# A two-layer hybrid block on one core: four more feed-forward chunks by seven block products, raw weights in half tiles, and a turn of the activations without steps

## The chip, the cores and the metric

The kernel runs on one core of one Trainium2 chip. The metric is the device time of one execution in microseconds (us), as the median of several runs; lower is better. The names of the engines are those of the profile: PE is TensorE (matmuls), PEld its weight loads, DVE is VectorE, ACT is ScalarE, POOL is GpSimd, SP is SyncE, which here issues nearly all DMA transfers in one order.

## What is computed

Two layers over 256 tokens of width 1024, all in float32. Each layer has two feed-forward nets, and between them a mixer and a cross attention that the change touches only through its smaller pieces. Every part is followed by a residual sum and a layer norm:

```python
def swiglu(x, w_gate, w_up, w_down):
    return (jax.nn.silu(x @ w_gate) * (x @ w_up)) @ w_down

for l in range(DEPTH):                      # DEPTH = 2
    h = layer_norm(ALPHA * h + 0.5 * swiglu(h, ffn1_gate[l], ffn1_up[l], ffn1_down[l]), ...)
    ...                                     # mixer, then cross attention
    h = layer_norm(ALPHA * h + 0.5 * swiglu(h, ffn2_gate[l], ffn2_up[l], ffn2_down[l]), ...)
```

The hidden width of a net is 2816, so a net has five chunks of 512 hidden columns (chunks 0 to 4) and a last one of 256 (chunk 5). There are four nets, called net 1 (ffn1 of the first layer) to net 4 (ffn2 of the second) below.

## The kernel before, in words

**Precision.** Every float32 factor is kept as two tiles of a faster matmul type, a high part and the rest. `split` (L60) makes them: ACT casts the source into the high part (L61), then DVE subtracts it from the source and writes the low part (L62). A product is three matmuls: high by high, high by low, low by high (`mm_rows`, L130; the matmul itself is L106). For weights the two parts are 128x1024 tiles named whi and wlo. One such pair is called a *piece* here. There are 8 buffers of whi and of wlo, so that a piece can only be cast when PE has done with the piece eight before it.

**Weights.** `load` (L64) brings 1 MB (128x2048) at a time into a tile named raw, of which there are three, by one DMA from SP, and splits it into two pieces. A raw tile is free again when both its pieces are split. The down weights of chunks 0 to 4 are read so that a partition takes neighbouring rows (`strewn`, L78).

**A net** (`ffn`, L376) goes through the chunks in order (L639). In a usual chunk (`hidden`, L484, and `first`, L424, for chunk 0) gate and up are each 8 blocks of 128 rows, in 4 pieces each; a piece serves 12 matmuls. With the two token tiles that is 96 matmuls of 512 columns. SiLU and the product of gate and up (`activate` L401, `gated` L404) leave an activation of tokens by columns, which `turn` (L411) brings into columns by tokens: four DMAs deal it among the partitions (L415), two DVE transposes of 32x32 blocks turn it (L418), and `split` makes its two parts (ah, al). After chunk c come the down products of chunk c-2, second half, and of chunk c-1, first half (`both`, L631: two pieces and 24 matmuls each). The last three slabs of down weights run token tile by token tile in `finish` (L292) with the layer norm.

**Seven products.** In nets 2 to 4 chunk 3 goes through `by_seven` (L515): token tiles, halves of the input rows, and gate and up form a 2x2 block product, which is done with 7 block products in place of 8, each of 12 matmuls: 84 in place of 96. Each of the 7 needs 2 pieces, which serve 6 matmuls each, so there are 14 pieces in place of 8. Four of the block products take sums of weight blocks. They are made in place, one after the other, by DVE (L544, 8 additions of 128x1024). Sums of x are made beforehand by `blocks_of_x` (L497) in a tile named quarters and put into kTh and kTl; in the code it stands behind chunk 1. The results are put together by DVE (L566). The raw blocks lie in: a tile "spare" that the quarters have used before (w00), the tiles of the layer norm's factors (w01), and two raw tiles (w11, w10).

**What sets the order.** Each engine runs its own instructions strictly in the order of the built program. That order is made by a scheduler at build time, from the code's order and its own estimate of costs; it is fixed when the kernel runs. SP's transfers too are one queue in that order.

Of the kernel before, what the change touches and what calls it, by code (L numbers as in the profile page):

```python
# [17 lines left out]
P = 128  # L18
# [28 lines left out]
def model(ctx: ExitStack, tc: tile.TileContext, t: dict, out: bass.AP):  # L47
# [16 lines left out]
    def load(src, k0, nk, c0, ncol, fine=False, strewn=False):  # L64

        hi, lo, todo = [], [], []
        step = 2048 // ncol
        for a in range(k0, k0 + nk, step):  # L70
            raw = wp.tile([P, 2048], F32, tag="raw", name="raw", bufs=3)
            raw = raw.rearrange("p (k c) -> p k c", c=ncol)
            half = step // 2
            part = 1 if fine else step
            for b in range(0, step, part):
                loads.append(nc.sync.dma_start(
                    raw[:, b : b + part, :],
                    src[:, c0 : c0 + ncol].rearrange("(p k) c -> p k c", p=P)[:, a + b : a + b + part, :]  # L78
                    if strewn
                    else src[(a + b) * P : (a + b + part) * P, c0 : c0 + ncol].rearrange("(k p) c -> p k c", p=P),  # L80
                ))
            for s in range(2):
                h = wp.tile([P, 1024], F32R, tag="whi", name="whi", bufs=8)
                w = wp.tile([P, 1024], F32R, tag="wlo", name="wlo", bufs=8)
                h = h.rearrange("p (k c) -> p k c", c=ncol)
                w = w.rearrange("p (k c) -> p k c", c=ncol)
                r = raw[:, s * half : (s + 1) * half, :]
# [65 lines left out]

    jdn = cst.tile([P, P], F32, name="jdn")
# [24 lines left out]
    def load_memory(mp, behind):  # L179
        m = [mp.tile([P, 4, 8, 32], F32, tag="m", name="m", bufs=2) for _ in range(2)]  # L180
# [23 lines left out]
    rows = cst.tile([P, P], F32, name="rows")  # L204
# [10 lines left out]
    def small_parameters(op):  # L215
        nc.gpsimd.memset(rows, 0.0)
# [13 lines left out]
        mf = op.tile([P, NT, len(narrow), 64], F32, name="mf", bufs=1)  # L230
# [61 lines left out]
    def finish(mm, y, scale, gb, last=False, flip=False):  # L292
# [6 lines left out]
        for i in range(NT):  # L299
# [8 lines left out]
            for c in pieces:  # L308
# [6 lines left out]
                else:  # L315
                    mm(
                        i, n, slice(0, 512), None,
                        None if last or not i or not n else lambda: transposed(h[0], 0, xTh, xTl),
# [21 lines left out]
        return lambda: transposed(h[1], 1, xTh, xTl, jdn if flip else idn)  # L340

    def project_back(slabs, late, gb, scale, between=lambda: None):
# [30 lines left out]
        return finish(tail, y, scale, gb)  # L373


    def ffn(l, name, n, pend=None, last=False, early=None):  # L376
        gate, up, down = (t[f"{name}_{x}"][l] for x in ("gate", "up", "down"))
        with tc.tile_pool(name="ffn", bufs=2, reuse_waits="tile") as fp:
# [21 lines left out]

            def activate(s, i, og):  # L401
                nc.scalar.activation(halves(s[:, i, :]), sums(og), AF.Silu)

            def gated(s, i, ou):  # L404
                v = halves(s[:, i, :])
                nc.vector.tensor_tensor(v, sums(ou), v, op=ALU.mult)
# [4 lines left out]
            def turn(s):  # L411
# [4 lines left out]
                for i in range(NT):  # L416
                    d = fp.tile([P, 4, P], F32, tag="up", name="square")
                    nc.vector.transpose(  # L418
                        d.rearrange("p k (i b) -> p b k i", b=4), x[:, :, i, :].rearrange("p b (j k) -> p b k j", k=4)
# [4 lines left out]
            def first():  # L424
# [5 lines left out]
                if pend is None:  # L430
# [8 lines left out]
                    with tc.manual_schedule(engines={E.Activation, E.DVE, E.PE}):  # L439
# [8 lines left out]
                        transposed_half(h[0], 0, 0, xTh, xTl)  # L448
                        busy(1)
                        split(*wg.todo[0])  # L450
                        transposed_half(h[0], 0, 1, xTh, xTl)
# [3 lines left out]
                        transposed_half(h[1], 1, 0, xTh, xTl)  # L455
                        group(1, 0)
                        split(*wg.todo[2])
                        transposed_half(h[1], 1, 1, xTh, xTl)
# [38 lines left out]
            def blocks_of_x():  # L497

                d = fp.tile([P, 4, 4 * P], F32, tag="spare", name="quarters", bufs=1)
                q = [d[:, n, :].rearrange("p (k t) -> p k t", t=P) for n in range(4)]  # L500
# [14 lines left out]
            def by_seven(c0, bx):  # L515
                def quarter(m, j, halves_of):
                    for b, r in enumerate(halves_of):
                        n = r.shape[1]
                        k = 4 * j + b * n
                        loads.append(nc.sync.dma_start(  # L520
                            r, m[k * P : (k + n) * P, c0 : c0 + CHUNK].rearrange("(k p) c -> p k c", p=P)
                        ))
                    return [r[:, 2 * h : 2 * h + 2, :] for h in range(2) for r in halves_of[:1]] if n == 4 else halves_of

# [3 lines left out]
                def raw():  # L528
                    return rows_by_columns(wp.tile([P, 2048], F32, tag="raw", name="raw", bufs=3))
# [4 lines left out]
                w01 = quarter(up, 0, [  # L534
                    rows_by_columns(wp.tile([P, DM], F32, tag=g, name="raw")) for g in ("lng", "lnb")
                ])
                w11 = quarter(up, 1, [raw()])
                w10 = quarter(gate, 1, [raw()])

                def parts_of(r, plus=None):  # L540
                    hi, lo = [], []
                    for i in range(2):
# [4 lines left out]
                        h, w = (x.rearrange("p (k c) -> p k c", c=CHUNK) for x in (h, w))  # L547
# [14 lines left out]
                def half_sum():  # L562
                    return halves(fp.tile([P, 4, P], F32, tag="up", name="half").rearrange("p k t -> p (k t)"))

                def put(o, a, op, b):
                    nc.vector.tensor_tensor(o, a, b, op=op)  # L566

                s = activations()
                g = [halves(s[:, i, :]) for i in range(NT)]
                o = [acc((P, CHUNK)) for _ in range(4)]  # L570
                run(o[0], part_of_x(0, 0), parts_of(w00))
                nc.scalar.copy(g[0], sums(o[0]))
# [3 lines left out]
                put(e, sums(o[1]), ALU.add, g[0])  # L576
                run(o[3], bx[2], parts_of(w01, w11))
                put(g[1], sums(o[3]), ALU.add, e)
                f = half_sum()
                put(f, sums(o[2]), ALU.subtract, g[1])  # L580
                put(e, sums(o[2]), ALU.subtract, e)
# [12 lines left out]
                put(g[0], g[0], ALU.mult, e)  # L594
                return turn(s)

            def last_hidden(c0):
# [11 lines left out]
                split(ah[:, 0:2, :], al[:, 0:2, :], s)  # L609
# [11 lines left out]
            sevens = (3,) if early is None else ()  # L621
# [17 lines left out]
            for c, (c0, ncol) in enumerate(chunks):  # L639
# [7 lines left out]
                if c == 1 and sevens:  # L647
                    bx = blocks_of_x()
                if c == (max(sevens) + 1 if sevens else 1):

                    with tc.issue_after(loads[-1].ins) if early is not None else nullcontext():
                        gb = ln_params(l, n)
                        rest = early(fp) if early is not None else ()
# [19 lines left out]
            return finish(tail, ys, 0.5, gb, last=last, flip=name == "ffn1")  # L673
# [27 lines left out]
    def mixer(l, fill):  # L701
        w_in = t["w_in"][l]
        with tc.tile_pool(name="mix", bufs=1, reuse_waits="tile") as mp:
# [284 lines left out]
            return project_back([slab(a) for a in (0, 6, 2, 4)], 3, gb, 1.0)  # L988


    def attention(l, pend):
        scale = (DM // HEADS) ** -0.5
        with tc.tile_pool(name="att", bufs=1, reuse_waits="tile") as ap:
# [108 lines left out]
            return project_back([slab(a) for a in (0, 2, 4, 6)], 3, gb, 1.0, others)  # L1102
# [40 lines left out]
```

## Time and profile before

| what | us |
|---|---|
| median of 3 runs (lowest, highest) | 1081.91 (1081.46, 1082.29) |
| the profiled execution's own time | 1082.44 |
| its span in the profile | 1080.7 |
| PE busy | 1071.4 (99%) |
| DVE busy | 908.4 (84%) |
| ACT busy | 592.8 (55%) |
| mean traffic of the DMA engines | 215 GB/s |

Times inside the profile count from the start of the span. A group of instructions is given with its line, engine, operation, "out<-in" by the program's tile names, a shape and a count; then its busy time in all, the mean duration of one in ns, and the idle time of the engine just before it with what ended that. A row of a timeline has start, length, engine, line, operation and count, and in brackets the idle time before it. Two DVE instructions in a row overlap a little, so that the distance from start to start is shorter than the duration of one.

### The profile page before, as it was taken

The numbers are of one execution on the slowest core, as the hardware profiler recorded it, in microseconds if no ns is written. First come the engines' busy times: TensorE is split into PE (matmuls) and PEld (weight loads), VectorE is DVE, ScalarE is ACT, GpSimd is POOL, SyncE is SP. The second block draws the span as 40 slices with busy tenths as digits, with TensorE's granted clock in tenths as the row PEclk, the third lists the DMA queues.
The fourth block names the chain that finished last, engine by engine and source line by source line (L and its number), as shares of the span: only waits on it lengthen the run. The fifth ranks groups of instructions, "written<-read, shape, count | busy, mean of one in ns | idle before, by whom it ended". The sixth has DMA issues, their size and how long they took to land.

```text
span 1080.7 us, 15689 instructions
## 1 busy us (share of the span) xinstructions
PE 1071.4 (99%) x6015; PEld 947.5 (88%) x6015; DVE 908.4 (84%) x1198; ACT 592.8 (55%) x828; POOL 61.0 (6%) x113
## 2 busy tenths in 40 slices
PE   9999999999999999999999999999999999999997
PEld 7888888989899888888888888898898998888886
DVE  6678677998988898998697998798989889889885
ACT  6456553766457455556365465456764664645650
POOL 9500001000000000000000000010000000000000
PEclk9999999999999999999999999999999999999999
DMA  9986764754476387288468459656536664773761
GB/s 325 289 293 203 249 223 153 237 196 165 167 263 204 123 295 269 96 275 286 156 234 282 166 166 329 229 165 241 174 122 231 240 228 154 255 253 109 260 236 39
DMA packets 122715, 231.86 MB, mean 215 GB/s; under 512 B 6352, under 2 KB 45552, under 8 KB 117520
## 3 DMA queue, kind: packets, MB, share of 16 engines
q1 hardware_dynamic: 120848, 228.48, 63.1%
q0 software_dynamic: 1216, 1.20, 0.4%
q10 hardware_dynamic: 576, 1.18, 0.3%
q8 instruction: 47, 0.77, 0.3%
q14 instruction: 28, 0.23, 0.1%
HBM read 216.15 MB, written 1.05 MB: 201 GB/s over the span
## 4 chain that ended last, share of the span: by engine, by line
PE 99%; DMA 0%; DVE 0%; issue 0%; DVEq 0%
PE acc L106 65%; PE dn L106 30%; PE acc L170 1%; PE dn L845 1%; DMA h<-in_x_dram 0%; PE dn L904 0%; PE dn L903 0%; PE dn L893 0%; PE acc L969 0%; PE dn L810 0%; PE dn L437 0%; DVE h L334 0%; DVE h L330 0%; DVE st L322 0%; DVE h L314 0%
## 5 line engine op out<-in xcount | busy, mean ns | idle before, releaser
L62 DVE TENSOR_TENSOR wlo<-raw,whi 128x1024 fp32r<-128x1024 f32 (+1 forms) x390 | 460.8, 1207 | 91.0 <-ACT whi L61 81.1
L61 ACT CAST whi<-raw 128x1024 fp32r<-128x1024 f32 (+1 forms) x390 | 391.2, 1040 | 258.3 <-PE dn L106 128.4
L106 PE MATMUL acc<-whi,xT 128*128 128x512 f32 x1192 | 359.7, 380 | 0.0
L106 PEld LDWEIGHTS acc<-whi,xT 128*128 128x128 f32 x1192 | 225.2, 189 | 32.1
L106 PE MATMUL acc<-wlo,xT 128*128 128x512 f32 x596 | 225.9, 379 | 0.0
L106 PE MATMUL acc<-xT,whi 128*128 128x512 f32 x576 | 142.1, 382 | 0.0
L106 PE MATMUL dn<-whi,ah 128*128 128x512 f32 x346 | 131.5, 380 | 0.0
L106 PE MATMUL dn<-wlo,ah 128*128 128x512 f32 x346 | 131.2, 379 | 0.0
L106 PE MATMUL dn<-whi,al 128*128 128x512 f32 x346 | 131.1, 379 | 0.0
L106 PEld LDWEIGHTS acc<-wlo,xT 128*128 128x128 f32 x596 | 112.7, 189 | 15.7
L106 PEld LDWEIGHTS acc<-xT,whi 128*128 128x128 f32 x576 | 104.1, 190 | 11.8
L106 PE MATMUL dn<-whi,xT 128*128 128x512 f32 x288 | 88.8, 382 | 0.0
L106 PEld LDWEIGHTS acc<-xT,wlo 128*128 128x128 f32 x576 | 75.5, 191 | 3.9
L106 PE MATMUL acc<-xT,wlo 128*128 128x256 f32 x576 | 75.9, 275 | 0.0
L106 PEld LDWEIGHTS dn<-wlo,ah 128*128 128x128 f32 x346 | 65.4, 189 | 9.5 <-DVE wlo L62 0.3
L106 PEld LDWEIGHTS dn<-whi,al 128*128 128x128 f32 x346 | 65.4, 189 | 9.3
L106 PEld LDWEIGHTS dn<-whi,ah 128*128 128x128 f32 x346 | 65.4, 189 | 9.1
L418 DVE STREAM_TRANSPOSE square<-dealt 128x512 f32<-128x512 f32 x40 | 62.8, 1645 | 3.8 <-DMA dealt<-sg 3.8
L327 POOL TENSOR_TENSOR rs<-rs,nhalf 128x1 f32<-128x1 f32 x16 | 14.9, 928 | 846.3 <-DVE rs L326 846.3
L106 PEld LDWEIGHTS dn<-whi,xT 128*128 128x128 f32 x288 | 54.7, 190 | 7.8 <-DVE xT L62 0.3
L106 PE MATMUL dn<-wlo,xT 128*128 128x512 f32 x144 | 54.8, 381 | 0.0
L61 ACT CAST ah<-square 128x512 fp32r<-128x512 f32 x40 | 24.6, 619 | 39.7 <-DVE square L418 39.7
(227 smaller groups left out, 1174.0 us busy)
## 6 DMA issues: line engine op xcount, KB each, us to landing
raw<-in_ffn_down_dram SPq DMA_DIRECT2D x44, 1024.0 KB, 5.4
raw<-in_ffn_up_dram SPq DMA_DIRECT2D x41, 1024.0 KB, 6.1
raw<-in_ffn_gate_dram SPq DMA_DIRECT2D x39, 1024.0 KB, 5.1
raw<-in_w_in_dram SPq DMA_DIRECT2D x24, 1024.0 KB, 5.0
dealt<-sg SPq DMA_DIRECT2D x80, 128.0 KB, 3.8
raw<-in_ca_k_dram SPq DMA_DIRECT2D x8, 1024.0 KB, 4.9
raw<-in_w_out_dram SPq DMA_DIRECT2D x8, 1024.0 KB, 4.8
raw<-in_ca_v_dram SPq DMA_DIRECT2D x8, 1024.0 KB, 5.4
```

The lines of the kernel that those rows point to most:

```text
L61: nc.scalar.copy(hi, src)
L62: lows.append(nc.vector.tensor_tensor(lo, src, hi.bitcast(F32), op=ALU.subtract))
L106: nc.tensor.matmul(o, w, x, start=start, stop=stop)
L170: nc.tensor.transpose(pt[:, k, :], src[:, (4 * j + k) * P : (4 * j + k + 1) * P], unit)
L327: nc.gpsimd.tensor_tensor(rs, rs, nhalf[:, 0:1], op=ALU.pow)
L418: nc.vector.transpose(d.rearrange("p k (i b) -> p b k i", b=4), x[:, :, i, :].rearrange("p b (j k) -> p b k j", k=4))
L845: nc.tensor.matmul(o[g, hh, :], kc[:, hh, g], x, start=True, stop=True)
```

## The change

In four parts:

1. **Which chunks go by seven products.** Nets 2 to 4: chunks 2 and 4 in place of chunk 3. Net 1: chunk 4 in place of none. In nets 2 to 4 `blocks_of_x` still stands behind chunk 1; in net 1 behind chunk 2. Inside `by_seven` the block product with w11 alone comes before the two with w10, and the activation is written into a tile of its own, with SiLU from the sums and then one product per token tile.
2. **Raw weights.** Six tiles of 128x1024 in place of three of 128x2048, each filled by a transfer of its own (512 KB). `strewn` is gone: all weights are read row block by row block. The blocks of `by_seven` are single half tiles too; w00 lies in the quarters' two tiles (nets 2 to 4) or in raw (net 1).
3. **The turn.** The order of the hidden columns is chosen so that the transposes read and write runs of 32 neighbouring elements in place of every fourth. For this `activate` and `gated` write the activation in another order and in two instructions of 128x256 each. The order of rows that `strewn` gave the down weights is no longer needed.
4. **A permuted identity** `pdn`, made by POOL, with which x is turned before a net, and which is made before the first transposes.

```diff
-    def load(src, k0, nk, c0, ncol, fine=False, strewn=False):
+    def load(src, k0, nk, c0, ncol, fine=False):
...
-            raw = wp.tile([P, 2048], F32, tag="raw", name="raw", bufs=3)
-            raw = raw.rearrange("p (k c) -> p k c", c=ncol)
             half = step // 2
-            part = 1 if fine else step
+            raw = [
+                wp.tile([P, 1024], F32, tag="raw", name="raw", bufs=6).rearrange("p (k c) -> p k c", c=ncol)
+                for _ in range(2)
+            ]
+            part = 1 if fine else half
...
+    pdn = cst.tile([P, P], F32, name="pdn")
+    nc.gpsimd.tensor_copy(pdn.rearrange("p (r b) -> p b r", b=4), idn.rearrange("p (b r) -> p b r", b=4))
...
+            def ordered(v):
+                return v.rearrange("p (a k j) -> p k a j", a=4, j=32)
+
+            def by_two(v, o):
+                o = o.rearrange("p (n a j m) -> p m n a j", n=2, a=4, m=2)
+                return [(ordered(v)[:, 2 * m : 2 * m + 2], o[:, m]) for m in range(2)]
+
             def activate(s, i, og):
-                nc.scalar.activation(halves(s[:, i, :]), sums(og), AF.Silu)
+                for v, o in by_two(s[:, i, :], og):
+                    nc.scalar.activation(v, o, AF.Silu)
 
             def gated(s, i, ou):
-                v = halves(s[:, i, :])
-                nc.vector.tensor_tensor(v, sums(ou), v, op=ALU.mult)
+                for v, o in by_two(s[:, i, :], ou):
+                    nc.vector.tensor_tensor(v, o, v, op=ALU.mult)
...
                     nc.vector.transpose(
-                        d.rearrange("p k (i b) -> p b k i", b=4), x[:, :, i, :].rearrange("p b (j k) -> p b k j", k=4)
+                        d.rearrange("p k (b r) -> p b k r", b=4), x[:, :, i, :].rearrange("p b (k j) -> p b k j", k=4)
                     )
...
-                w00 = quarter(gate, 0, [rows_by_columns(
-                    fp.tile([P, 4, 4 * P], F32, tag="spare", name="sum", bufs=1).rearrange("p n c -> p (n c)")
-                )])
...
+                w00 = block(gate, 0, pieces("spare0", "spare1") if early is None else pieces("raw", "raw"))
+                w01 = block(up, 0, pieces("lng", "lnb"))
+                w11 = block(up, 1, pieces("raw", "raw"))
+                w10 = block(gate, 1, pieces("spare2", "raw") if early is None else pieces("spare0", "spare1"))
...
-                m = acc((P, CHUNK))
-                run(m, part_of_x(0, 1), parts_of(w10))
-                put(g[0], sums(m), ALU.add, g[0])
-                nc.scalar.activation(g[0], g[0], AF.Silu)
-                m = acc((P, CHUNK))
-                run(m, part_of_x(1, 1), parts_of(w00, w10))
-                put(g[1], sums(m), ALU.add, g[1])
-                nc.scalar.activation(g[1], g[1], AF.Silu)
-                put(g[1], g[1], ALU.mult, f)
-                m = acc((P, CHUNK))
-                run(m, bx[3], parts_of(w11))
-                put(e, sums(m), ALU.add, e)
-                put(g[0], g[0], ALU.mult, e)
+                o = [acc((P, CHUNK)) for _ in range(3)]
+                run(o[0], bx[3], parts_of(w11))
+                put(e, o[0], ALU.add, e)
+                run(o[1], part_of_x(0, 1), parts_of(w10))
+                put(g[0], o[1], ALU.add, g[0])
+                run(o[2], part_of_x(1, 1), parts_of(w00, w10))
+                put(g[1], o[2], ALU.add, g[1])
+                s = fp.tile([P, NT, CHUNK], F32, tag="spare2", name="sg", bufs=1)
+                for i, u in enumerate((e, f)):
+                    v = ordered(s[:, i, :])
+                    nc.scalar.activation(v, g[i].rearrange("p (k a j) -> p k a j", a=4, j=32), AF.Silu)
+                    nc.vector.tensor_tensor(v, v, u.rearrange("p (k a j) -> p k a j", a=4, j=32), op=ALU.mult)
                 return turn(s)
...
-                if c < len(chunks) - 1:
-                    w = load(down[c * CHUNK : (c + 1) * CHUNK], 2 * u, 2, 0, DM, strewn=True)
-                else:
-                    w = load(down, c * 4, 2, 0, DM)
+                w = load(down, c * 4 + 2 * u, 2, 0, DM)
...
-            sevens = (3,) if early is None else ()
+            sevens = (2, 4) if early is None else (4,)
...
-                if c == 1 and sevens:
+                if sevens and c == 1 and early is None:
                     bx = blocks_of_x()
...
                 if c == 2 and early is not None:
                     with tc.issue_after(lows[-1].ins):
                         for f in rest:
                             f()
+                    if sevens:
+                        bx = blocks_of_x()
```

More of the change, by code (lines that the diff above doesn't have):

```diff
@@ L86, in load @@
                 w = w.rearrange("p (k c) -> p k c", c=ncol)
-                r = raw[:, s * half : (s + 1) * half, :]
+                r = raw[s]
                 if fine:
@@ L179, in load_memory @@
     def load_memory(mp, behind):
-        m = [mp.tile([P, 4, 8, 32], F32, tag="m", name="m", bufs=2) for _ in range(2)]
+        m = [
+            mp.tile([P, DM], F32, tag=f"spare{n}", name="m", bufs=1).rearrange("p (k b j) -> p k b j", k=4, j=32)
+            for n in range(2)
+        ]
         with tc.issue_after(behind.ins):
@@ L317, in finish @@
                         i, n, slice(0, 512), None,
[L318 removed]
+                        None if last or not i or not n else lambda: transposed(h[0], 0, xTh, xTl, units[0]),
                     )
@@ L339, in finish, with project_back @@
                     e.dma_start(out[0, tok(i), c], h[i][:, c])
-        return lambda: transposed(h[1], 1, xTh, xTl, jdn if flip else idn)
-    def project_back(slabs, late, gb, scale, between=lambda: None):
+        return lambda: transposed(h[1], 1, xTh, xTl, units[1])
+    def project_back(slabs, late, gb, scale, unit, between=lambda: None):
         y = [[acc((P, 512), "dn") for _ in range(2)] for _ in range(NT)]
@@ L497, in blocks_of_x @@
             def blocks_of_x():
-                d = fp.tile([P, 4, 4 * P], F32, tag="spare", name="quarters", bufs=1)
-                q = [d[:, n, :].rearrange("p (k t) -> p k t", t=P) for n in range(4)]
+                d = [fp.tile([P, DM], F32, tag=f"spare{n}", name="quarters", bufs=1) for n in range(2)]
+                q = [d[n // 2].rearrange("p (n k t) -> p n k t", n=2, t=P)[:, n % 2] for n in range(4)]
                 for n, (i, j) in enumerate(((1, 0), (1, 1), (0, 0), (0, 1))):
@@ L671, in tail @@
                         rows_of(a, i, k, m, first, u == 2 and k == 1, cols, alone)
-            return finish(tail, ys, 0.5, gb, last=last, flip=name == "ffn1")
+            return finish(tail, ys, 0.5, gb, (idn, jdn) if name == "ffn1" else (pdn, pdn), last=last)
     def keys(l, c, between={}):
```

87 lines of the change are left out of this document (45 added, 42 removed).

## The prediction, made before the run

> **What bounds the kernel now.** I read the page first (busy shares and the chain that ended last), then the chain in order of time, PE's waits, DVE's timeline around the seven products, DVE's groups by shape, and the transfers.
>
> ```profile
> PE 1071.4 (99%) x6015; PEld 947.5 (88%) x6015; DVE 908.4 (84%) x1198; ACT 592.8 (55%) x828; POOL 61.0 (6%) x113
> PE 99%; DMA 0%; DVE 0%; issue 0%; DVEq 0%
> ```
>
> ```profile
> 10.57 9.22 PE dn L106 x42
> ...
> 118.31 20.72 PE acc L106 x96
> 139.03 10.36 PE dn L106 x48
> ...
> 419.84 20.72 PE acc L106 x96
> 440.56 10.36 PE dn L106 x48
> 450.92 18.13 PE acc L106 x84
> ```
>
> ```profile
> PE dn L437 <- DVE kTh L432: 1.5, 1, 1.5
> PE acc L170 <- DMA h<-in_x_dram: 0.6, 1, 0.6
> ```
>
> PE is the whole chain, and it is dense: 96 matmuls in 20.72 us are 0.216 us each, 84 in 18.13 are 0.216 as well, and each piece of the chain begins where the one before ends. PE's only waits are two at the start. So two things follow. A matmul less is worth 0.216 us, in full. And any wait that the change gives PE costs its full length, since nothing can be caught up.
>
> **What the change removes from PE.** A chunk by seven products has 84 matmuls in place of 96: 12 x 0.216 = 2.59 us. Nets 2 to 4 gain one such chunk each, net 1 one: 4 x 2.59 = **-10.4 us**. Everything else on PE keeps its count.
>
> **What it adds on DVE.** The prices:
>
> ```profile
> L62 DVE TENSOR_TENSOR wlo<-raw,whi 128x1024 fp32r<-128x1024 f32 x382 | 455.5, 1217 | 91.0 <-ACT whi L61 81.1 <-PE acc L106 8.2
> L418 DVE STREAM_TRANSPOSE square<-dealt 128x512 f32<-128x512 f32 x40 | 62.8, 1645 | 3.8 <-DMA dealt<-sg 3.8
> L544 DVE TENSOR_TENSOR sum<-sum,raw 128x1024 f32<-128x1024 f32 x18 | 21.5, 1221 | 0.2
> L127 DVE TENSOR_TENSOR sums<-acc,sums 128x256 f32<-128x256 f32 x32 | 13.3, 419 | 2.5 <-ACT sums L126 2.5
> L980 DVE STREAM_TRANSPOSE yr<-dealt 128x512 f32<-128x512 f32 x4 | 4.7, 1287 | 0.0
> L1054 DVE STREAM_TRANSPOSE square<-dealt 128x512 f32<-128x512 f32 x6 | 4.2, 705 | 0.0
> ```
>
> ```profile
> 440.01 0.68 DVE L406 TENSOR_TENSOR sg<-acc,sg 128x512 f32<-128x512 f32 x1
> 440.61 1.22 DVE L62 TENSOR_TENSOR wlo<-sum,whi 128x1024 fp32r<-128x1024 f32 x1
> 441.74 0.68 DVE L406 TENSOR_TENSOR sg<-acc,sg 128x512 f32<-128x512 f32 x1
> ```
>
> From start to start, a 128x512 operation takes 0.60 us and a 128x1024 one 1.135, about 0.08 less than their durations; so I count 0.34 for 128x256. The new transposes aren't in this trace. Those of L1054 read and write runs of 32 and take 705 ns, those of L980 write every fourth element and take 1287, those of today 1645. The new pattern is L1054's, so I take 0.62 from start to start; the other end, no gain, is 1.57. A half of `gated` lies between 0.34 and 0.60; its size is that of L127, so 0.34.
>
> A chunk by seven needs 14 subtractions, 8 additions, 7 combinations, 2 products, the turn (2 transposes, 2 subtractions) and 4 subtractions for the down pieces after it: 26 x 1.135 + 11 x 0.60 + 2 x 0.62 = 37.4 us of DVE, while PE needs 18.13 + 10.36 = 28.5. A usual chunk needs 12 x 1.135 + 4 x 0.34 + 2 x 0.62 + 2 x 0.60 = 17.4 us against 31.1. So on average DVE can follow, but a seven lives on a lead of about 9 us that DVE must have built up. The lead can't exceed eight pieces, which in a seven are 8 x 6 x 0.216 = 10.4 us of PE.
>
> Over the program the sum on DVE is smaller than the free share: 4 chunks x 20 us more, less 40 transposes x 0.94, some 40 to 55 us on 908 of 1081. What counts is where the lead stands, so I follow DVE's order through each seven.
>
> **Today's seven, as a check.**
>
> ```profile
> 433.95 1.23 DVE L62 TENSOR_TENSOR wlo<-sum,whi 128x1024 fp32r<-128x1024 f32 x1 [0.93 <-ACT whi L61]
> ```
>
> ```profile
> 462.38 0.67 DVE L566 TENSOR_TENSOR half<-acc,sg 128x512 f32<-128x512 f32 x1
> 462.99 2.34 DVE L62 TENSOR_TENSOR wlo<-raw,whi 128x1024 fp32r<-128x1024 f32 x2
> ```
>
> DVE begins its pieces at 433.95, 17 us ahead of PE (450.92), as soon as a buffer is free, and has subtracted the 14th at 465.3. PE takes a piece every 6 x 0.216 = 1.295 us and wants the 14th at 450.92 + 13 x 1.295 = 467.8: 2.5 us to spare. Only one of the seven combinations stands before the last piece.
>
> **Nets 2 to 4, chunk 2.** Two things take the lead away. First, w00 lies where the quarters lie, as before, but its chunk comes one earlier, so that its transfer waits for their last reader:
>
> ```profile
> 400.63 0.68 DVE L62 TENSOR_TENSOR kTl<-quarters,kTh 128x512 fp32r<-128x512 f32 x1
> 401.23 1.22 DVE L62 TENSOR_TENSOR wlo<-raw,whi 128x1024 fp32r<-128x1024 f32 x1
> 404.94 2.36 DVE L62 TENSOR_TENSOR wlo<-raw,whi 128x1024 fp32r<-128x1024 f32 x2 [2.49 <-ACT whi L61]
> ```
>
> ```profile
> raw<-in_ffn_down_dram SPq DMA_DIRECT2D x44, 1024.0 KB, 5.4
> ...
> raw<-in_w_out_dram SPq DMA_DIRECT2D x8, 1024.0 KB, 4.8
> ...
> raw<-in_ffn_up_dram SPq DMA_DIRECT2D x6, 512.0 KB, 4.0
> ```
>
> ```profile
> L61 ACT CAST whi<-raw 128x1024 fp32r<-128x1024 f32 x382 | 386.6, 1049 | 258.3 <-PE dn L106 128.4 <-PE acc L106 42.3 <-DMA raw<-in_ffn_up_dram 29.1
> ```
>
> The quarters are free at 401.3; SP holds nothing else back by then. 4.0 us for a 512 KB transfer puts w00's first half at about 405.3 and its second 1.3 us later; with a cast of 1.05 each, DVE starts on the second piece at 408.2. That is 11.6 us ahead of PE, which comes to chunk 2 at 419.84 whatever happens, in place of 17. Second, the order: in the built program there stand, from that piece to the last of the 14, 21 operations of 128x1024, nine of 128x512 (six combinations and one product among them), four halves of `gated` and two transposes, and the last sum is behind the fourth of PE's results. 21 x 1.135 + 9 x 0.60 + 4 x 0.34 + 2 x 0.62 = 31.8, and 0.6 for a cast between the last addition and its subtraction: 408.2 + 32.4 = 440.6. PE wants it at 419.84 + 13 x 1.295 = 436.7, and 0.2 for the high part and 0.4 for two down matmuls that the order puts ahead: 437.3. So PE waits **about 3.4 us, in each of the three nets**. Nothing is late before it by more than 0.5 us.
>
> **Nets 2 to 4, chunk 4.** Ahead of it lies a usual chunk, the quarters aren't in the way, and the buffers let DVE begin 17 us ahead again. By the same ledger the last piece comes 1.8 us before it is wanted, and the down pieces behind it 0.9: no wait.
>
> **Net 1, chunk 4.** w00 lies in raw and could be early, but in the built order its two subtractions stand behind both token tiles' `gated` of chunk 3. Those wait for PE's end of that chunk, 118.31 + 20.72 = 139.03 by the chain; today's pair begins before that and ends after it:
>
> ```profile
> 138.71 1.28 DVE L406 TENSOR_TENSOR sg<-acc,sg 128x512 f32<-128x512 f32 x2
> ```
>
> So DVE starts at about 139.8, and PE at 139.03 + 10.36 = 149.4: a lead of 9.6. To the last piece: 22 x 1.135 + 9 x 0.60 + 2 x 0.62 + 0.6 = 32.2, so 172.0. Wanted: 149.4 + 16.84 + 0.6 = 166.8. PE waits **about 5.2 us**.
>
> **What costs nothing.** pdn is made after jdn (which ends at 1.74). A copy of 128x128 isn't in the trace; jdn's own pass over 128x128 takes 0.30 us, and even five times that is hidden, since the first transposes wait for x until 4.66:
>
> ```profile
> 1.44 0.30 POOL L156 TENSOR_SCALAR_AFFINE_SELECT jdn<-jdn 128x128 f32<-128x128 f32 x1
> ...
> 4.66 1.09 PE L170 MATMUL acc<-idn,h 128*128 128x128 f32 x4 [0.63 <-DMA h<-in_x_dram]
> ```
>
> In net 1 the 1 MB of w01 is now fetched at the very start, ahead of the second half of up. At the 325 GB/s of the page's first slice it delays that by 3.2 us; today those pieces are done by 21.1 and wanted after two of up's four, at 19.78 + 2 x 2.59 = 25.0:
>
> ```profile
> GB/s 325 289 293 203 249 223 153 237 196 165 167 263 204 123 295 269 96 275 286 156 234 282 166 166 329 229 165 241 174 122 231 240 228 154 255 253 109 260 236 39
> ```
>
> ```profile
> 18.69 2.40 DVE L62 TENSOR_TENSOR wlo<-raw,whi 128x1024 fp32r<-128x1024 f32 x2 [0.47 <-ACT whi L61]
> ```
>
> That leaves 0.7 us, and without that cover it would cost up to 3. The 19.78 is where the first piece of the chain above ends (10.57 + 9.22). Half tiles double SP's weight transfers but let each go out one piece earlier. The down weights are now read by row block as w_out's are, which land in 4.8 us against 5.4: no price.
>
> **The sum.** -10.4 + 3 x 3.4 + 5.2 = **+5.0 us** on the span of 1080.7, so 1085.7. The profiled execution took 1082.44, 1.74 more than its span and 0.53 above the median of 1081.91; on the median that is 1086.9.
>
> **The rivals.**
>
> *The lead holds (faster).* The ledger hangs on DVE's start. If the quarters are free by 398 in place of 401.3, because half tiles bring chunk 1's weights sooner and DVE isn't held up, w00 lands in time and nets 2 to 4 lose nothing: -10.4 + 5.2, 1076.7. If net 1 keeps up too, 1071.5. The point is a mean wait of 2.6 us per net. For it: DVE was idle 2.49 us at 402.4 today. Against it: between 369 and 401 its timeline shows nearly no gap, and those instructions remain. Chance of over 0.2% faster: 0.21.
>
> *Waits and gain cancel.* If the four waits sum to 8 to 12.5 us, the time is within 0.2% (2.2 us) of today's, about what a measurement of this kernel can tell from no change: 0.15.
>
> *The transposes don't get cheaper* (the turn doesn't do what it says). At 1287 ns as in L980, a pair takes 1.2 us more inside each of the four ledgers: +4.7, 1091.6. Chance 0.07.
>
> *The clock drops in the gaps.* At the start, before PE has been busy for long, matmuls of 512 columns take twice as long:
>
> ```profile
> 7.03 0.85 PE dn L437 x2
> ```
>
> 0.425 us each, against 0.216 later. The slow state still holds at 7.9 us and no longer at 10.6. If a gap of some 2.5 us puts PE back into it for 3 to 7 us (an estimate from those two), each of the four waits costs 1.7 to 3.4 us more: 1094 to 1100. Chance 0.08. The Trainium skill, "TensorE: Matmul & The Clock Gate", section "What's actually happening", has a rule for this: the clock halves after an idle window of about 3.4 us. By that rule the longest single gap of my ledgers (2.3 us) is too short; no run here shows such a gap yet.
>
> *My forecast*: 1084 to 1090, chance 0.49.
>
> **How the numbers follow.** Faster 0.21, same 0.15, slower 0.64 (0.49 + 0.07 + 0.08). The range reaches down to where net 1 alone waits and up past the slow transposes into the lower half of the clock's case: 1076 to 1095, with about 0.1 left out on either side.
>
> **What would show it.** PE's first entry of waits is a DVE L62 wlo near the end of four sevens, one per net; the chain's pieces of acc in chunk 2 of nets 2 to 4 are 21 to 22 us long in place of 18.13, in chunk 4 they are 18.13. The transposes show near 705 ns. I am wrong if PE's waits stay near 2 us in all, or if a wait stands in chunk 4 of nets 2 to 4, or if matmuls after a wait take 0.43 us.

## The result, and the profile after

The changed kernel takes **1096.62 us** (median of 4 runs, 1093.02 to 1098.9), the kernel before 1081.68: ratio 1.0134, 95% interval 1.0106 to 1.0162. It is slower, as forecast, but by 14.9 us in place of 5.0, and just outside the range. The profiled execution is the fastest of the four: 1093.02 us, a span of 1091.3 against 1080.7, 10.6 us more. The runs differ in one thing that the results list, the mean granted clock of PE: 0.994 in the profiled one, then 0.991, 0.991 and 0.988; the kernel before has 0.998.

The page of the changed kernel, engines and the chain by engine:

```profile
PE 1068.9 (98%) x5967; PEld 940.1 (86%) x5967; DVE 962.9 (88%) x1324; ACT 622.6 (57%) x890; POOL 63.3 (6%) x114
```

PE has 48 matmuls less and is no longer the whole chain. Its waits (engine, line, what it waited for: total, times, longest):

```profile
PE acc L105 <- ACT whi L61: 9.1, 6, 2.1
PE acc L105 <- DVE wlo L62: 1.8, 5, 0.4
PE dn L105 <- ACT whi L61: 1.6, 4, 0.5
```

These are waits for weight pieces that weren't there before. Where they stand, the chain in order of time tells (start, length, what). A few pieces of the changed kernel:

```profile
19.04 31.08 PE acc L105 x144
...
117.57 6.43 PE acc L105 x30
...
143.20 9.93 PE dn L105 x46
...
185.20 7.86 PE acc L105 x48
...
447.21 9.93 PE dn L105 x46
...
488.22 18.13 PE acc L105 x84
...
516.71 10.48 PE acc L105 x64
...
661.54 18.13 PE acc L105 x84
...
690.03 10.48 PE acc L105 x64
...
1023.86 18.13 PE acc L105 x84
...
1052.35 10.48 PE acc L105 x64
```

and the pieces at the same places of the kernel before that the prediction doesn't show:

```profile
181.47 7.86 PE acc L106 x48
...
510.49 10.48 PE acc L106 x64
...
681.10 10.48 PE acc L106 x64
...
1042.18 10.48 PE acc L106 x64
```

Chunk 4 of nets 2 to 4 is dense: three pieces of 84 in 18.13 us. Net 1's seven begins at 117.57, is dense for 30 matmuls and then broken up; in chunk 2 of nets 2 to 4 no piece of 84 is left at all. From the differences after less before at the five places (-0.74, 3.73, 6.22, 8.93, 10.17 us) each net's own loss follows, with the 2.59 us that its seven saves added back: net 1 7.06, net 2 5.08, net 3 5.30, net 4 3.83. With 0.4 us in the tail, -0.74 - 10.36 + 21.27 + 0.43 = 10.6: the whole difference.

Three nets do the same work, and their losses differ by up to 1.5 us. PE's timeline shows why. Net 2, end of chunk 2:

```profile
440.73 0.38 PE L105 MATMUL acc<-whi,xT 128*128 128x512 f32 x1
443.22 0.71 PE L105 MATMUL acc<-whi,xT 128*128 128x512 f32 x1 [2.12 <-ACT whi L61]
444.17 1.22 PE L105 MATMUL dn<-whi,ah 128*128 128x512 f32 x2 [0.24 <-ACT whi L61]
445.19 0.63 PE L105 MATMUL acc<-wlo,xT 128*128 128x512 f32 x1
445.61 1.06 PE L105 MATMUL acc<-whi,xT 128*128 128x512 f32 x2
```

and net 4, the same place:

```profile
977.63 0.38 PE L105 MATMUL acc<-whi,xT 128*128 128x512 f32 x1
980.13 0.48 PE L105 MATMUL acc<-whi,xT 128*128 128x512 f32 x1 [2.12 <-ACT whi L61]
981.07 0.70 PE L105 MATMUL dn<-whi,ah 128*128 128x512 f32 x2 [0.46 <-ACT whi L61]
981.61 0.38 PE L105 MATMUL acc<-wlo,xT 128*128 128x512 f32 x1
981.83 0.59 PE L105 MATMUL acc<-whi,xT 128*128 128x512 f32 x2
```

The wait is the same 2.12 us. Behind it net 2's matmuls start 0.42 to 0.43 us apart (445.19 to 445.61), net 4's 0.22. The view by windows (start and end, length, PE busy with the count of matmuls, granted clock, DMA share, GB/s) names the cause; the first three windows are net 2's, the last two net 4's:

```profile
439.93:443.34 3.41, 1.29 (x6) 1.00 0.61 166
443.34:446.75 3.41, 3.17 (x7) 0.50 0.78 217
446.75:450.16 3.41, 3.41 (x17) 1.00 0.99 359
975.82:979.23 3.41, 1.75 (x7) 1.00 0.44 117
979.23:982.64 3.41, 2.05 (x8) 1.00 0.72 205
```

In net 2 the clock is at 0.50 for 3.41 us, one such stretch, and as long in nets 1 and 3. A stretch costs up to half its length, 1.71 us. Net 4 has none, so its 3.83 us are the wait alone. Net 1's stretch (129.31 to 132.72) lies ahead of its longest wait, so that most of what it cost was taken off that wait; c_net1 below shows how much.

### The profile page after: what moved, and what is told of

The parts are those of the page before. It is cut to its first block, busy times and chain, and to the rows that moved or that the text cites. A ratio compares the mean times of both kernels' runs of the same rounds, so it can differ in the third digit from the quotient of the medians.

```text
span 1091.3 us, 16307 instructions
## 1 busy us (share of the span) xinstructions
PE 1068.9 (98%) x5967; PEld 940.1 (86%) x5967; DVE 962.9 (88%) x1324; ACT 622.6 (57%) x890; POOL 63.3 (6%) x114
## 4 chain that ended last, share of the span: by engine, by line
PE 76%; DVE 16%; issue 4%; DMA 2%; ACT 1%; SPq 0%; DVEq 0%; ACTq 0%
PE acc L105 47%; PE dn L105 27%; DVE wlo L62 6%; DVE raw L562 3%; DMA raw<-in_ffn_down_dram 2%; DVE half L584 1%; PE acc L172 1%; DVE sg L422 1%; DVE h L340 1%; DVE quarters L520 1%; DVE kTl L62 1%; DVE h L326 1%; PE dn L866 1%; DVE xT L62 0%; DVE h L336 0%
## 5 line engine op out<-in xcount | busy, mean ns | idle before, releaser
L61 ACT CAST whi<-raw 128x1024 fp32r<-128x1024 f32 (+1 forms) x438 | 439.3, 1042 | 256.2 <-DVE raw L562 92.1
L62 DVE TENSOR_TENSOR wlo<-raw,whi 128x1024 fp32r<-128x1024 f32 (+1 forms) x438 | 515.0, 1207 | 51.6 <-ACT whi L61 46.5
L105 PE MATMUL acc<-whi,xT 128*128 128x512 f32 x1032 | 315.7, 382 | 7.9 <-ACT whi L61 7.9
L105 PEld LDWEIGHTS acc<-whi,xT 128*128 128x128 f32 x1032 | 195.9, 190 | 37.5 <-ACT whi L61 9.5
L105 PE MATMUL acc<-wlo,xT 128*128 128x512 f32 x516 | 196.9, 382 | 1.5 <-DVE wlo L62 1.5
L105 PEld LDWEIGHTS acc<-wlo,xT 128*128 128x128 f32 x516 | 98.1, 190 | 16.8 <-DVE wlo L62 3.1
L562 DVE TENSOR_TENSOR raw<-raw 128x1024 f32<-128x1024 f32 x56 | 66.0, 1215 | 0.1
L333 POOL TENSOR_TENSOR rs<-rs,nhalf 128x1 f32<-128x1 f32 x16 | 14.9, 930 | 854.0 <-DVE rs L332 854.0
L105 PE MATMUL acc<-whi,kTh 128*128 128x512 f32 x112 | 42.9, 383 | 1.2 <-ACT whi L61 1.2
```

The lines of the kernel that those rows point to most:

```text
L61: nc.scalar.copy(hi, src)
L62: lows.append(nc.vector.tensor_tensor(lo, src, hi.bitcast(F32), op=ALU.subtract))
L105: nc.tensor.matmul(o, w, x, start=start, stop=stop)
L333: nc.gpsimd.tensor_tensor(rs, rs, nhalf[:, 0:1], op=ALU.pow)
L562: nc.vector.tensor_tensor(r[i], r[i], plus[i], op=ALU.add)
```

## The experiments

**Theory 1**: DVE brings the last pieces of four sevens late, and PE waits; nothing else of the change costs anything. **Theory 2**: on top of that the gaps make PE's clock fall, 1.7 us each time, and how often differs from run to run. **Rival**: half tiles, transfers or the turn cost time themselves. Comparisons are with the kernel before on the same chip, 1081.5 to 1081.6 us.

| kernel | us (runs) | ratio, 95% interval |
|---|---|---|
| a_old_sevens | 1081.63 (1081.53 to 1082.19) | 0.9991 to 1.001 |
| b_nets24 | 1091.73 (1090.0 to 1093.42) | 1.0075 to 1.0108 |
| c_net1 | 1087.28 (1086.21 to 1088.23) | 1.0035 to 1.0065 |
| d_nets24_filled | 1086.49 (1085.76 to 1087.5) | 1.0029 to 1.0059 |
| m1_defer | 1085.42 (1085.22 to 1086.23) | 1.0024 to 1.0051 |
| m2_inside | 1078.54 (1077.8 to 1079.84) | 0.9961 to 0.9984 |
| m12 | 1076.76 (1076.15 to 1077.27) | 0.9942 to 0.9968 |
| m3_rawq | 1083.57 (1083.18 to 1084.76) | 1.0009 to 1.0028 |
| t_twice | 1106.07 (1105.44 to 1109.83) | 1.0218 to 1.0251 |
| m12_nets24 | 1075.82 (1075.16 to 1076.16) | 0.9932 to 0.9957 |
| m123_nets24 | 1073.98 (1073.77 to 1074.28) | 0.9916 to 0.9943 |

### Which part costs

```diff
-            sevens = (2, 4) if early is None else (4,)
+            sevens = (3,) if early is None else ()        # a_old_sevens
+            sevens = (2, 4) if early is None else ()      # b_nets24
+            sevens = (3,) if early is None else (4,)      # c_net1
```

> The changed kernel with the old choice of sevens: one in nets 2 to 4 (chunk 3), none in net 1. The new turn, the half tiles with their own transfers, the new order of the down weights and pdn stay. Theory 1 (what was lost is PE waiting for late pieces at the end of the added sevens): those waits go with the sevens, so 1081.7 less the 0.6 us by which the dense part now starts earlier: about 1081, all runs within 0.5 us, PE's waits near 2 us in all. Rival (the half tiles, the transfers or the turn cost something themselves): a part of the 15 us stays, 1084 or more.

> Two sevens (chunks 2 and 4) in nets 2 to 4, none in net 1. Theory 1: 1081.7 - 0.6 - 3 x 2.59 + the waits of the changed kernel's profile in chunk 2 (about 3.6 each at full clock) = 1084.1. Theory 2 (on top of the waits, PE's clock halves for about 3.4 us after some of the gaps, 1.7 us each time, and how often differs from run to run): between 1084.1 and 1089.2 with a spread of some us between runs, and steps of about 1.7 us. Theory 1 alone: 1084.1 in every run.

> One seven in nets 2 to 4 (chunk 3, as before) and one in net 1 (chunk 4). Theory 1: 1081.7 - 0.6 - 2.59 + 5.3 (net 1's wait at full clock) = 1083.8. Theory 2: 1083.8 to 1087.2, by one or two drops of the clock of 1.7 us. If net 1's loss came from elsewhere (the memory's work beside it), it would still be here, but PE's waits would not be put down to whi and wlo.

a_old_sevens is as fast as the kernel before: everything but the added sevens costs and gains nothing, and the rival falls. (The dense part starts 0.7 us earlier than in the profile of the kernel before, but that doesn't show in the time. It probably belongs to that one run: its matmuls at 8.10 and 8.53 still stand 0.43 us apart, those of the changed kernel at 7.92 and 8.14 only 0.22, and its 1082.44 us is 0.76 above the median.) b_nets24 loses 10.10 against a_old_sevens, or with the 7.77 saved added back 5.96 us in each net; that is above the whole interval that theory 2 gave. Its trace has four steps at half clock, two of them in net 4. c_net1 loses 5.65, so net 1 alone costs 8.24; its time lies at the upper end of theory 2's interval. Its only stretch at half clock ahead of the last microseconds (141.56 to 144.97) comes behind the last wait for a whi, so that it shows net 1's wait at full clock. The end of that wait in the changed kernel, then in c_net1:

```profile
140.47 0.48 PE L105 MATMUL acc<-whi,xT 128*128 128x512 f32 x1 [1.55 <-ACT whi L61]
```

```profile
140.01 0.48 PE L105 MATMUL acc<-whi,xT 128*128 128x512 f32 x1 [1.54 <-ACT whi L61]
```

The dense part of c_net1 starts 0.14 us earlier (18.90 against 19.04), so the stretch ahead of that point cost the changed kernel only 0.3 us in net 1, and the wait by itself is 7.06 - 0.3 = 6.7 us. Net 1 and nets 2 to 4 together lose 15.75, and the changed kernel lies 14.99 above a_old_sevens: the parts add up to within 0.8.

### The gap filled with useless work

```diff
                     for k in range(4):
                         wh, wl = w.at(k, slice(0, CHUNK))
+                        if k == 2 and idle:
+                            blank = acc((P, CHUNK))
+                            for _ in range(idle):
+                                product(blank, x[0][:, 1, :], w.at(1, slice(0, CHUNK))[0], True, True)
...
-                run(o[2], part_of_x(1, 1), parts_of(w00, w10))
+                run(o[2], part_of_x(1, 1), parts_of(w00, w10), 9 * (c0 == 2 * CHUNK))
```

> b_nets24 with nine matmuls of 128x512 whose result nobody reads, put in front of the late piece of chunk 2's last product in nets 2 to 4. They work on the piece before it, so they run in the gap of 2.1 us (9 x 0.216 = 1.94) and PE isn't idle there. Theory 2 with the idle time as the cause: the clock stays at 1.00 behind the gaps, every run is at 1084 to 1084.6, and the spread goes. Theory 1 alone, or a clock that falls for another reason: times and clocks as b_nets24's, or some tenths above. If the gaps were smaller than thought, up to 5.8 us are added.

With 27 matmuls more, whose result nobody reads, the kernel is **5.2 us faster** than b_nets24, and the mean clock goes from 0.990 to 0.995 up to 0.998 to 0.999. PE's timeline of d_nets24_filled, net 2:

```profile
436.17 2.32 PE L105 MATMUL acc<-whi,xT 128*128 128x512 f32 x10
438.67 0.48 PE L105 MATMUL acc<-whi,xT 128*128 128x512 f32 x1 [0.17 <-ACT whi L61]
439.61 0.70 PE L105 MATMUL dn<-whi,ah 128*128 128x512 f32 x2 [0.46 <-ACT whi L61]
440.15 0.38 PE L105 MATMUL acc<-wlo,xT 128*128 128x512 f32 x1
440.36 0.59 PE L105 MATMUL acc<-whi,xT 128*128 128x512 f32 x2
```

The ten matmuls are the last real one and the nine idle ones; the wait of 2.12 is down to 0.17, and the matmuls behind it start 0.21 us apart. The piece is just as late, so what went is the clock's part: 5.2 / 3 = 1.75 us a net, about one stretch each; the trace has no stretch at half clock before its last microseconds. What is left, (1086.49 - 1081.63 + 7.77) / 3 = 4.2 us a net, is nearly all the wait (3.8 to 4.0 a net in the profiled run). The median is about 2 above the 1084 to 1084.6 expected, since that had 3.6 us for a wait and took 0.6 off for the early start. A spread of 1.7 us between its runs stays, at the same clock; its cause is open.

### The clock by itself

```diff
+    for r in range(REPEATS):        # 9
+        for m in range(LENGTHS):    # 8
+            n = 50 + 7 * ((3 * r + m) % REPEATS)
+            for k in range(n):
+                nc.tensor.matmul(o, s, w, start=k == 0, stop=k == n - 1)
...
+            for _ in range(m):
+                nc.vector.tensor_tensor(y, v, h[0][:, 512:], op=ALU.add)
...
+            nc.vector.scalar_tensor_tensor(s, v[:, 0:P], 0.0, h[0][:, 0:P], op0=ALU.mult, op1=ALU.add)
```

> A kernel of its own, nothing of the reference is computed: PE runs dense rows of 50 to 106 matmuls of 128x512 (10.8 to 22.9 us); between two rows PE waits for a chain of zero to seven additions of 128x512 and one small operation on DVE, so that gaps of about 0.4, 1.0, 1.6, 2.2, 2.8, 3.4, 4.0 and 4.6 us come nine times each, at ever other times. Theory 2: behind gaps of some length the matmuls take 0.43 us in place of 0.216 for about 3.4 us; never behind the shortest, always behind the longest, and between them it depends on where the gap falls. Rival (the clock falls by itself, for the load or the heat): drops come behind gaps of every length alike, or inside the dense rows.

Gaps between the rows came out at 0.38, 1.11, 1.84, 2.66, 3.29, 4.02, 4.74 and 5.47 us. A fall of the clock followed in 0 of 9, 0 of 9, **0 of 9, 9 of 9**, 7 of 9, 9 of 9, 9 of 9 and 8 of 8. So theory 2 holds and its rival falls: there is none behind a short gap and none inside a row. One gap of 2.66 us in the timeline of p_gaps, and the clock around it:

```profile
71.61 4.68 PE L69 MATMUL acc<-w,s 128*128 128x512 f32 x13 [2.66 <-DVE s L76]
```

```profile
69.59:73.00 3.41, 1.39 (x6) 1.00 0.00 0
73.00:76.42 3.42, 3.42 (x9) 0.50 0.00 0
```

All falls start on one grid of 3.413 us and last one or two of its steps. Laid over the 71 gaps, that grid gives a sharp rule: the clock fell after each of the 42 gaps that had 2.02 us or more of idle time inside one step, and after none of the 29 with 1.92 or less. The two gaps of 3.29 us without a fall lay across a border, 1.86 + 1.42 and 1.92 + 1.37. It is not the gap's length that decides, but how much of it lies in one step. The grid isn't tied to the kernel: net 1's stretch starts at 129.31 in the changed kernel and at 130.02 in m3_rawq. In the changed kernel net 2's gap left 2.12 idle in the step 439.93 to 443.34, and the next step ran at 0.50; net 4's was cut by a border (1.66 and 1.36 idle) and nothing fell. So a kernel with gaps near 2 us can spread.

The border in idle time holds for the probe, where a step has one gap. Net 1 of the changed kernel had 3.41 - 1.88 = 1.53 us idle in a step, in three gaps, and the clock fell; net 3 of m1_defer (below) had 1.58 in a step, and it didn't:

```profile
125.90:129.31 3.41, 1.88 (x7) 1.00 0.43 154
129.31:132.72 3.41, 3.41 (x9) 0.50 0.52 165
```

```profile
608.63:612.04 3.41, 1.83 (x6) 1.00 0.49 135
612.04:615.45 3.41, 3.04 (x14) 1.00 0.90 291
```

The profile shows a matmul as 0.38 us or more long, though in a dense row one starts every 0.216 us, so each gap looks some 0.2 us shorter than the time in which PE had nothing to do. With 0.216 us for each matmul, the two steps are 2.23 and 2.12 us short of work, and the traces of all the kernels agree with the probe: no step at full clock with less than 2.10 us brought a fall, each one with 2.16 or more did, and between these three did and four didn't.

### DVE's order and lead

m1_defer writes two combinations behind the last product; m2_inside puts half of the down products ahead of it; m12 does both.

```diff
                 run(o[0], bx[3], parts_of(w11))
-                put(e, o[0], ALU.add, e)
                 run(o[1], part_of_x(0, 1), parts_of(w10))
-                put(g[0], o[1], ALU.add, g[0])
+                between()
                 run(o[2], part_of_x(1, 1), parts_of(w00, w10))
+                put(e, o[0], ALU.add, e)
+                put(g[0], o[1], ALU.add, g[0])
```

In m2_inside and m12 `between` issues both(c - 2, 1), which no longer stands behind the seven; in m1_defer that line is not there, and in m2_inside the two `put` stay.

> The changed kernel with two of the seven's combinations (into e and g[0]) written behind the last product, so that on DVE the last sum stands ahead of them and the product with silu behind the last subtraction. Theory 1 (the waits are DVE's ledger): the last piece comes about 1.2 us earlier in each of the four sevens that wait, so 1096.6 - 4 x 1.2 = 1091.8. Theory 2 (the clock's drops on top): some of the drops go as well, 1086 to 1092. If the waits were set by something else than DVE's order, 1096.6.

> The changed kernel with the first half of the down products (24 matmuls, 5.18 us of PE) put ahead of each seven's last product. PE comes to the late pieces 5.18 us later; DVE has two subtractions more in front of them (2.27 us). Theory 1: the wait of about 3.8 us shrinks to 0.9 or less in nets 2 to 4 and from about 6 to 3 in net 1: 1081.6 - 10.4 + 3 x 0.9 + 3 = 1077; with theory 2 nearly no drop of the clock is left, at most one or two, 1077 to 1080. If seven products are slow for another reason, it stays above 1090.

> Both edits of the order together (combinations behind the last product, half of the down products ahead of it). Theory 1: no wait in nets 2 to 4, some 2 us in net 1: 1081.6 - 10.4 + 2 = 1073, and with theory 2 hardly a drop of the clock, so runs within 1 to 2 us of each other. The floor without any wait is 1071.2.

m1_defer's waits for whi, for comparison with the 9.1 us and 2.1 longest above:

```profile
PE acc L105 <- ACT whi L61: 5.0, 6, 0.9
```

The longest wait shrinks from 2.1 to 0.9, 1.2 as expected; four times that is 4.8 us. The nets bear it out: counted as above they lose 5.5, 2.7, 2.8 and 2.6 us, against 6.7 and three times 3.83 at full clock. The time fell by 11.2. The other 6.4 are put down to falls of the clock that no longer come: the profiled run has none ahead of its last microseconds, and the mean clock is 0.996 to 0.998. m2_inside and m12 come out 1.5 and 3.8 us above their point forecasts; in m12 net 1 still loses 3.4 us and net 4 1.2, nets 2 and 3 only 0.2 each.

```diff
-                w00 = block(gate, 0, pieces("spare0", "spare1") if early is None else pieces("raw", "raw"))
+                w00 = block(gate, 0, pieces("raw", "raw") if early is not None or c0 == 2 * CHUNK else pieces("spare0", "spare1"))
...
-                w10 = block(gate, 1, pieces("spare2", "raw") if early is None else pieces("spare0", "spare1"))
+                w10 = block(gate, 1, pieces("spare0", "spare1") if early is not None or c0 == 2 * CHUNK else pieces("spare2", "raw"))
```

> The changed kernel, but in chunk 2 w00 goes into two raw tiles (as in net 1) and w10 into the two that held the quarters, so that the first block's transfer needn't wait for the quarters' last reader. The prediction's step (the transfer takes 5.4 us of DVE's lead): the waits of nets 2 to 4 go, 1081.6 - 10.4 + 8 = 1079 to 1081. Rival (DVE is full by then, it stands idle only 0.44 us in front of w00's first subtraction and 1.3 us around the turn, so an earlier transfer gives little): 1 us less in each of three nets at most, 1091 to 1096.

Here the rival that I had come to believe falls: 13 us less, though 2.6 above the interval by the prediction's step. DVE's timeline of the changed kernel in net 2, then that of m3_rawq:

```profile
410.73 2.36 DVE L62 TENSOR_TENSOR wlo<-raw,whi 128x1024 fp32r<-128x1024 f32 x2 [0.44 <-ACT whi L61]
...
436.08 1.21 DVE L562 TENSOR_TENSOR raw<-raw 128x1024 f32<-128x1024 f32 x1
...
440.83 1.21 DVE L562 TENSOR_TENSOR raw<-raw 128x1024 f32<-128x1024 f32 x1
...
443.20 3.50 DVE L62 TENSOR_TENSOR wlo<-raw,whi 128x1024 fp32r<-128x1024 f32 x3 [0.56 <-ACT whi L61]
```

```profile
406.74 1.23 DVE L62 TENSOR_TENSOR wlo<-raw,whi 128x1024 fp32r<-128x1024 f32 x1 [0.18 <-ACT whi L61]
...
437.02 1.22 DVE L562 TENSOR_TENSOR raw<-raw 128x1024 f32<-128x1024 f32 x1
...
441.78 1.22 DVE L62 TENSOR_TENSOR wlo<-raw,whi 128x1024 fp32r<-128x1024 f32 x1
```

DVE begins with w00 4 us earlier, and the last sum stands at 437.02 in place of 440.83: the built order has one of the two sums already done, so the cast of the last piece no longer waits behind the combinations. DVE gained only some 1.4 us at the last subtraction (441.78 in place of 443.20), and nets 2 to 4 still lose 1.7 us each in place of 3.83. That was enough to keep the clock up there: its trace has one fall, in net 1. Since the edit changes the built order too, it doesn't say how much of this is the earlier transfer by itself.

t_twice runs each transpose of the turn a second time:

```diff
+                    for _ in range(2):
                         nc.vector.transpose(
```

> The changed kernel with every transpose of the turn done twice into the same tile: 1.25 us more of DVE per chunk, about what the old strided transposes cost more (1.9 us). Theory 1 with a slope of one: four waits longer by 1.25 each, 1096.6 + 5 = 1101.6, and perhaps some tenths in chunk 4 of nets 2 to 4, whose margin was forecast at 1.8 us. Theory 2: the gaps get longer, and the clock falls behind more of them, 1102 to 1107. If DVE weren't the bound there, 1096.6.

9.5 us more than the changed kernel, inside theory 2's interval. By the profiled runs the clock stands at 0.50 for six steps in place of three (up to 3 x 1.71 = 5.1 of 12.9 us); the rest is wait, and some of it is in chunk 4 of nets 2 to 4, where DVE's margin is now used up: 0.46 and 0.18 us in net 3. So the cheaper turn was worth something of this size to the change (the old turn itself wasn't run with it), though by a_old_sevens it is worth nothing without the added sevens.

### A version that beats both

> m12 without net 1's seven. In m12's trace nets 2 to 4 gain 2.4, 2.4 and 1.4 us against the kernel with the old choice of sevens, and net 1 loses 0.8 us. Theory 1: 1081.6 - 6.2 = 1075.4, 1.3 below m12. If net 1's seven gains something after all, it is 1077 or more.

> m12_nets24 with w00 in raw in chunk 2 as well. The floor with three added sevens and no wait is 1081.6 - 7.8 = 1073.8; m12_nets24 stands 2.0 above it, by waits of 0.2 to 0.9 us a net. Theory 1: the lead of about 2 us that w00 in raw gave DVE takes these away, 1073.8 to 1074.8. If the order inside has already used what DVE can give, 1075.8 again.

m12_nets24 takes 1075.82 us, 0.9 less than m12 and 0.4 above its forecast, so net 1's seven gained nothing there. m123_nets24 (two sevens in nets 2 to 4, none in net 1, both edits of the order, w00 in raw in chunk 2) takes **1073.98 us**, ratio 0.993 (0.9916 to 0.9943): 7.66 of the 7.77 us that three sevens can save. No weight piece is among its waits of PE:

```profile
PE dn L454 <- DVE kTh L449: 1.5, 1, 1.5
PE acc L172 <- DMA h<-in_x_dram: 0.5, 1, 0.5
```

## Why the prediction was right in its sign and wrong in its size

- **PE bounds, and a matmul is worth 0.216 us** (-10.4): right. m123_nets24 gets all of it where nothing waits.
- **Prices**: right. The transposes show 687 ns against the 705 taken, a half of `gated` 413 against 419.
- **Nets 2 to 4, chunk 2**: right in place and nearly in size; the entry of PE's waits is the cast (ACT whi) and not the subtraction (DVE wlo), since the cast of the last piece stands behind the last sum. The ledger ran from the second piece, 11.6 us ahead of PE's seven, to the end of the last subtraction 20.8 us after its start. The trace has 11.5 (411.87 against 423.40) and 20.9. The wait is 3.83 us against 3.4. Of the two causes named, the order is confirmed by m1_defer and m2_inside; m3_rawq took w00 from behind the quarters and shortened the loss by more than half, but changed the built order with it.
- **Chunk 4 of nets 2 to 4**: right, no wait.
- **Net 1**: right in mechanism, but read at the wrong rows. 139.03 is the end of chunk 4 of the kernel before; chunk 3 ends at 107.95. Since the chunks repeat every 31.08 us, the ledger moved over whole: DVE began its pieces at 109.05 behind `gated`, 8.5 us ahead of PE (9.6 forecast). The wait at full clock was 6.7 us against 5.2 forecast, and 1.1 of the difference is the shorter lead.
- **What costs nothing**: right as a whole, by a_old_sevens.
- **The step that failed is the sum**: "-10.4 + 3 x 3.4 + 5.2" prices a gap at its length and has no term for the clock behind it. The waits at full clock came to 6.7 + 3 x 3.83 = 18.2 against 15.4; with them alone the time would have been about 1089.5 (an estimate: 1081.68 - 10.4 + 18.2). The clock took 21.3 - 18.2 = 3.1 us more in the profiled run and, with the 3.6 us by which the median lies above it, about 6.7 in the median one. The prediction's own sign of this is there: matmuls behind the wait in net 2 take 0.43 us. The rival "the clock drops in the gaps" had the right price at its lower end (1.7 for each of four waits, 6.8) and the right times (1094 to 1100), but a chance of 0.08. That chance leaned on a rule: the Trainium skill, "TensorE: Matmul & The Clock Gate", section "What's actually happening", has the clock fall after an idle window of about 3.4 us, and section "HAM oscillation — how this bites in real kernels" asks for no idle gaps above that. The first also says that the window is 3413 ns and runs freely; the grid in p_gaps agrees with that. But a whole idle window isn't needed: in the probe 2.02 us of idle in 3.41 was enough each time. My own row, 0.425 us for matmuls at the start, said what a fall costs; no row said when it comes, and then 0.08 was too sure.

The median is 3.6 us above the profiled run. Its clock is lower by 0.003, and one step at 0.50 lowers the mean of a run of 1091 us by 0.5 x 3.41 / 1091 = 0.0016: two steps more, up to 3.4 us. This is an estimate, since only the profiled run has a trace, and mean clock and time don't always go together: two runs of m1_defer at 1085.22 and 1085.26 us have 0.998 and 0.996.

What stays open: why b_nets24 has an earlier gap in net 4 (1.38 us) that the changed kernel lacks; whether net 1's seven can be made to pay, which wasn't tried with w00's additions in another order.

## What to carry to other kernels

Price a new wait on a dense PE twice: its length, and up to 1.7 us for a clock that falls when about 2 us of idle time meet in one step of 3.4, several short gaps together as well as one long one. A ledger of one engine, instruction by instruction in the built order, forecast the wait to 0.4 us in nets 2 to 4 and to 1.5 in net 1; so use it to move the order until the wait is under a microsecond. 1.2 us less in each of four waits was worth 11.2 us here. If a gap can't be closed, matmuls that nobody reads can be worth their time.

## What the runs showed of the hardware that was not expected

- PE's granted clock is decided on a grid of 3.413 us. In the probe, after a step with 2.02 us idle or more (42 gaps) the next one runs at 0.50, with 1.92 or less (29 gaps) it doesn't. One gap of 2.66 us always did it (9 of 9), one of 1.84 never (0 of 9).
- Short gaps add up within a step: 0.76, 0.46 and 0.31 us in net 1, 1.53 together, brought the clock down. What counts is how little work the step had, not how long a gap was.
- Two gaps of 3.29 us did nothing because a border cut them in two.
- More work on PE made a kernel faster: 27 useless matmuls, 5.2 us.
